# Strassen's seven products for two thirds of a transformer's down projection

## The chip, the core and the metric

The kernel runs on one core of a Trainium2 chip. The core has a matrix engine (TensorE, PE in the profile; its weight loads are shown as PEld), VectorE (DVE), ScalarE (ACT), GpSimd (POOL), a queue engine (SyncE, SP), and 16 DMA engines that move data between memory (HBM) and the core's own memories SBUF and PSUM. The metric is the device time of one execution in microseconds (us).

## The reference

An encoder of two layers over 512 tokens and 16 meta tokens, width 1024. Each layer is a feed-forward block, a mixer (gated linear attention beside grouped-query attention) and a second feed-forward block:

```python
def swiglu(x, w_gate, w_up, w_down):
    return (jax.nn.silu(x @ w_gate) * (x @ w_up)) @ w_down
...
    for l in range(DEPTH):
        h = h + 0.5 * swiglu(rmsnorm(h, norm_gains[l, 0]),
                             ffn_w_gate[l, 0], ffn_w_up[l, 0], ffn_w_down[l, 0])
        h = h + mixer(rmsnorm(h, norm_gains[l, 1]), w_in[l], ...)
        h = h + 0.5 * swiglu(rmsnorm(h, norm_gains[l, 2]),
                             ffn_w_gate[l, 1], ffn_w_up[l, 1], ffn_w_down[l, 1])
    return rmsnorm(h, final_norm)[:, N_META:]
```

The change is in the four feed-forward blocks. Their hidden width is 2816, so that `w_gate` and `w_up` are 1024 x 2816 and `w_down` is 2816 x 1024; all is float32.

## The kernel before

**Layout and precision.** Activations lie transposed: 128 features on the partitions, tokens along the row (528, and 512 in the last block, where the meta tokens are dropped). The residual `h` is eight such tiles. Each operand of a matmul is split into a part rounded to the matrix engine's float32r format (`hi`) and the remainder (`lo`); a product is three matmuls, hi x hi, hi x lo and lo x hi.

**Weights.** The class `Weights` holds one plan of all loads in the order of use. SP loads a slab of 128 x 1024 (512 KB) up to nine loads ahead; `make` casts it to `whi` on ScalarE (L238) and takes the remainder `wlo` on VectorE (L239), three or four slabs ahead of use, in four buffers each.

**A feed-forward block** (`ffn`, L507) goes through the hidden width in 11 pairs of 256 features, in groups of 4, 4 and 3 pairs (`GROUPS`). `ffn_steps` (L50) writes its order out by hand.

For a pair, gate and up are computed by Strassen's method in Winograd's form: the weights of the pair are cut into four blocks, the tokens into two halves, and seven block products ("P" steps, 1 to 7) take the place of eight. A product has 24 matmuls (L531). The products need sums of weight blocks. `Weights.sums` makes them with DMAs: ScalarE negates a block (L184), and GpSimd's queue issues transfers that add to a tile in SBUF (L189). s3 is block 21 less block 11, s2 is block 22 plus s3, s4 is s2 less block 12, s1 is block 21 plus block 22; they serve products 7, 6, 3 and 5. Their tiles lie in two pools, `wsa` (three buffers, for s3 and s4) and `wsb` (two, for s2 and s1). The products run one pair into the next: 1 and 2 of the next pair stand between 7 and 4 of this one.

ScalarE and VectorE put the products together in snapshots (L537) and sums (L545, L553, L560). `hidden` (L563) scales by the norm's factor (L571), takes the Silu, multiplies by up (L577) and splits the result into hi and lo (L392, L393).

**The down projection** ("D" steps, `down`, L580) follows each group: for each of eight output tiles the 2 x 4 (or 2 x 3) hidden tiles of the group are multiplied with tiles of `w_down`, three matmuls each, in two halves of 264 tokens (in the last block one of 512). With four pairs that is 8 x 8 x 3 x 2 = 384 matmuls. So that TensorE needn't wait for the last pair's hidden tiles, the first four output tiles leave these for later (`HELD`). The accumulated tile is scaled by the norm's factor (L494) and added to `h` (L503): 16 VectorE instructions a group.

**Around it.** `Norm` makes the operands of the next block as soon as a tile of `h` is done. In the first block of each layer the output tiles of the third group feed the mixer, in the others the next block or the ending (L1057), which works in halves of the tokens. The order on each engine comes from a scheduler that follows the order of the program, but may bring an instruction forward that has all it needs.

Of the kernel before, what the change touches and what calls it, by code (L numbers as in the profile page):

```python
# [41 lines left out]
GROUPS = (4, 4, 3)  # L42
LATE = 5
HELD = 4
OPENING = ((0, 0), 0), ((0, 0), 1)
PLACE = {p: i for i, p in enumerate("1256743")}
# [3 lines left out]
def ffn_steps(opening):  # L50
# [4 lines left out]
    for g, n in enumerate(GROUPS):  # L55
# [6 lines left out]
        for i in range(n):  # L62
# [8 lines left out]
        steps += [("D", g, m, 0, 2 * n - 2) for m in range(2, HELD)]  # L71
        steps += [("D", g, m, 2 * n - 2, 2 * n) for m in range(HELD)]
        steps += [("D", g, m, 0, 2 * n) for m in range(HELD, KC)]
# [4 lines left out]
def weight_plan():  # L78
# [8 lines left out]
    def ffn(l, f):  # L87
        for step in ffn_steps((l, f) == (0, 0)):
            if step[0] == "P":
                plan.append(("op", (l, f)) + step[1:])  # L90
            else:
# [38 lines left out]

PLAN = weight_plan()
COLUMN, NSLAB = slab_columns(PLAN)
NPAIR = FF // P // 2
# [18 lines left out]
class Weights:  # L152
# [18 lines left out]
    def dram(self, f, i, name):  # L171
        return self.win[((f[0] * 2 + f[1]) * NPAIR + i) * 4 + ("11", "12", "21", "22").index(name)]

# [102 lines left out]
def build(tc, ctx, xt, wts, win, par, w2, const, umask, out):  # L276
# [10 lines left out]
    slots = {n: pool("s_" + n, b) for n, b in dict(g=16, t=6, rs=2).items()}  # L287
# [27 lines left out]
    def slot(tag, dtype=F32, n=None):  # L315
        return slots[tag].tile([P, T], dtype, tag=tag, name=nm(tag))[:, : n or live[0]]

# [71 lines left out]
    def split(src, tag_hi, tag_lo):  # L389
        n = src.shape[-1]  # L390
        hi, lo = slot(tag_hi, F32R, n), slot(tag_lo, F32R, n)
# [32 lines left out]
    class Norm:  # L424
# [58 lines left out]
        def rs(self):  # L483
# [6 lines left out]
            return rs  # L490
# [5 lines left out]
    def add_to_h(m, acc, rs, f):  # L496
        if rs is None:
            for pv, cut in acc.parts:
                V.tensor_tensor(cut(h(m)), cut(h(m)), pv, ALU.add)
        else:  # L500
# [6 lines left out]
    def ffn(l, f, norm, done, following):  # L507

        x, rs, n = norm.x, None, live[0]
        w = n // 2  # L510
        pools = open_pools("left", psum=("s2",), c=2, snap=3, s2=2)
        made, hid, sums = {}, {}, {}

        def product_of_pair(p, product):
# [19 lines left out]
            def snapshot(name):  # L534
                t = slots["snap"].tile([P, T], F32, tag="snap", name=nm("snap"))[:, :n]
                st[name] = v2(t)
                copied = S.copy(st[name], acc).ins  # L537
                W.behind = copied

            if product == "1":  # L540
                snapshot("p1")
            elif product == "2":
                c = slots["c"].tile([P, 4 * T], F32, tag="c", name=nm("c"))[:, : 4 * n]
                st["c"] = c.rearrange("p (j q c) -> p j q c", j=2, q=4)
                V.tensor_tensor(st["c"][:, :, 0], st["p1"], acc, ALU.add)  # L545
            elif product == "6":
                snapshot("q")
            elif apart:
                S.copy(st["c"][:, :, 2], acc)
                st["apart"] = True  # L550
            elif product == "7":
                snapshot("r")
                V.tensor_tensor(st["c"][:, :, 3], st["r"], st["Z"][:, :, :w], ALU.add)  # L553
                if "apart" in st:
                    V.tensor_tensor(st["c"][:, :, 2], st["c"][:, :, 2], st["r"], ALU.add)
# [3 lines left out]
            elif product == "3":  # L559
                V.tensor_tensor(st["c"][:, :, 1], st["q"], acc, ALU.add)  # L560
                hidden(st, p, 0)

        def hidden(st, p, m):  # L563

            c = st["c"]
            t, u = [c[:, j, 2 * m : 2 * m + 2].rearrange("p q c -> p (q c)") for j in range(2)]
# [6 lines left out]
            if pending:  # L573
                with after(prev_act[0]):
                    pending.pop()()
            for _, ud, _, us, cs in cuts:
                V.tensor_tensor(ud, t[:, cs], us, ALU.mult)  # L577
            hid[2 * p + m] = split(u, "g", "g")
# [623 lines left out]
```

## Time and profile before

| What | Value |
|---|---|
| runs, median (3 runs) | 2235.04 us (2234.63 to 2238.08) |
| profiled execution, first to last instruction | 2233.2 us |
| mean granted TensorE clock | 0.998 |
| TensorE, VectorE, ScalarE busy | 2196.7, 1519.1, 1195.1 us |
| read from HBM | 264.77 MB |
| the two mixers, roughly | 390 to 770 us and 1500 to 1870 us |

The span is that of the one execution that was profiled; the profile gives no other time for it, and the runs above are separate executions. In the rows of the profile, "L404 PE MATMUL ss<-g,whi" means line 404, engine, operation, written tile, read tiles. A mean in ns is that of one instruction. Where "idle before" stands, it is the time that the engine did nothing ahead of these instructions, with what ended it.

### The profile page before, as it was taken

The page shows a single profiled execution, that of the slowest core. Times are in us where ns is not written, and L with a number is a line of the kernel's source. Part 1 is how long each engine was busy: PE and PEld are TensorE (multiplying, and loading weights), DVE is VectorE, ACT ScalarE, POOL GpSimd, SP SyncE. Part 2 cuts the span into 40 slices and gives each one's busy share as a digit, 9 for nine tenths or more (in the row PEclk, how much of TensorE's full clock was granted, in tenths as well). Part 3 has the DMA queues.
Part 4 walks back from the last instruction along what each step waited for, and adds up shares of the span by engine and source line. Part 5 has one row for each costly group of instructions (what it writes and reads, how often), then busy time and mean ns, then how long its engine had stood idle before and what let it go on. Part 6 is the DMA issues. An engine that isn't in the chain of part 4 may idle for free.

```text
span 2233.2 us, 39696 instructions
## 1 busy us (share of the span) xinstructions
PE 2196.7 (98%) x16506; PEld 2091.9 (94%) x16506; DVE 1519.1 (68%) x2413; ACT 1195.1 (54%) x1771; POOL 154.2 (7%) x180
## 2 busy tenths in 40 slices
PE   7999999999999999999999999999999999999998
PEld 7999999989999999999999999999788888989897
DVE  7657567586876666565686565675878767756667
ACT  8536355354784564453575353553557836636453
POOL 1111010000000010101011110100000001101010
PEclk9999999999999999999999999999999999999999
DMA  9768563212113486776768686632121146868672
GB/s 275 206 157 221 152 164 106 76 53 72 48 39 114 133 201 168 171 195 154 198 152 207 154 204 167 165 109 77 54 79 48 48 123 156 221 161 207 168 182 67
DMA packets 88612, 315.58 MB, mean 141 GB/s; under 512 B 9840, under 2 KB 12272, under 8 KB 88432
## 3 DMA queue, kind: packets, MB, share of 16 engines
q1 hardware_dynamic: 61136, 218.26, 29.2%
q0 software_dynamic: 25344, 92.29, 23.2%
q8 instruction: 130, 2.13, 0.4%
q10 hardware_dynamic: 1952, 2.50, 0.3%
q14 instruction: 50, 0.41, 0.1%
HBM read 264.77 MB, written 2.10 MB: 120 GB/s over the span
## 4 chain that ended last, share of the span: by engine, by line
PE 79%; DVE 8%; DMA 6%; ACT 5%; issue 2%; SPq 0%; POOL 0%; DVEq 0%; ACTq 0%; POOLq 0%
PE ss L531 30%; PE ss L404 26%; PE mm L404 13%; DMA w<-win 4%; PE sm L404 2%; DVE wlo L239 2%; DMA s<-w 2%; PE sm L916 1%; ACT whi L238 1%; PE ss L891 1%; PE ss L410 1%; ACT t L387 1%; PE sm L932 1%; PE ss L892 1%; PE sm L933 1%
## 5 line engine op out<-in xcount | busy, mean ns | idle before, releaser
L531 PE MATMUL ss<-xc,whi 128*128 128x264 f32 (+1 forms) x4928 | 902.8, 285 | 13.3 <-ACT whi L238 7.4
L531 PEld LDWEIGHTS ss<-xc,whi 128*128 128x128 f32 x4928 | 766.2, 189 | 17.2 <-ACT whi L238 7.6
L531 PE MATMUL ss<-xc,wlo 128*128 128x264 f32 (+1 forms) x2464 | 701.8, 285 | 3.4 <-DVE wlo L239 3.4
L404 PE MATMUL ss<-g,whi 128*128 128x264 f32 (+2 forms) x2692 | 496.8, 300 | 1.6 <-ACT g L392 0.9
L531 PEld LDWEIGHTS ss<-xc,wlo 128*128 128x128 f32 x2464 | 465.7, 189 | 5.2 <-DVE wlo L239 5.0
L404 PEld LDWEIGHTS ss<-g,whi 128*128 128x128 f32 x2692 | 391.6, 188 | 19.1 <-ACT g L392 1.6
L404 PE MATMUL mm<-x,whi 128*128 128x264 f32 (+1 forms) x1712 | 384.7, 315 | 0.0
L239 DVE TENSOR_TENSOR wlo<-w,whi 128x1024 fp32r<-128x1024 f32 (+1 forms) x221 | 268.0, 1217 | 157.2 <-ACT whi L238 157.1
L238 ACT CAST whi<-raw 128x1024 fp32r<-128x1024 f32 x190 | 199.3, 1049 | 246.6 <-PE mm L404 97.5
L238 ACT CAST whi<-w 128x1024 fp32r<-128x1024 f32 (+1 forms) x221 | 229.8, 1046 | 160.0 <-PE ss L404 88.0
L404 PE MATMUL ss<-g,wlo 128*128 128x264 f32 (+2 forms) x1346 | 312.5, 300 | 0.0
L404 PEld LDWEIGHTS mm<-x,whi 128*128 128x128 f32 x1712 | 278.5, 188 | 16.5 <-issue 1.0
L239 DVE TENSOR_TENSOR wlo<-raw,whi 128x1024 fp32r<-128x1024 f32 x190 | 232.0, 1221 | 74.3 <-ACT whi L238 73.9
L404 PE MATMUL mm<-x,wlo 128*128 128x264 f32 (+1 forms) x856 | 266.3, 316 | 0.0
L404 PEld LDWEIGHTS ss<-g,wlo 128*128 128x128 f32 x1346 | 215.8, 188 | 8.2
L537 ACT COPY snap<-ss 128x528 f32<-128x528 f32 (+1 forms) x132 | 78.4, 594 | 221.0 <-PE ss L531 221.0
L404 PEld LDWEIGHTS mm<-x,wlo 128*128 128x128 f32 x856 | 159.7, 188 | 8.4 <-issue 0.7
L494 DVE SCALAR_TENSOR_TENSOR t<-ss,rs 128x528 f32<-128x528 f32 (+1 forms) x93 | 64.5, 701 | 125.5 <-PE ss L404 125.4
L239 DVE TENSOR_TENSOR wlo<-s,whi 128x1024 fp32r<-128x1024 f32 x88 | 107.5, 1222 | 32.9 <-ACT whi L238 32.9
L184 ACT ACTIVATE s<-w 128x1024 f32<-128x1024 f32 x88 | 92.1, 1057 | 53.2 <-DMA w<-win 37.7
L189 POOL DMA_DIRECT2D w<-win x44 | 38.9, 884 | 984.1 <-DMA w<-win 539.9
L238 ACT CAST whi<-s 128x1024 fp32r<-128x1024 f32 x88 | 92.5, 1051 | 0.0
(246 smaller groups left out, 2570.8 us busy)
## 6 DMA issues: line engine op xcount, KB each, us to landing
w<-win SPq DMA_DIRECT2D x219, 512.0 KB, 4.5
raw<-wts SPq DMA_DIRECT2D x190, 512.0 KB, 3.4
s<-win POOLq DMA_DIRECT2D x44, 512.0 KB, 7.1
w<-s POOLq DMA_DIRECT2D x44, 512.0 KB, 5.5
w<-win POOLq DMA_DIRECT2D x44, 512.0 KB, 5.9
s<-w POOLq DMA_DIRECT2D x44, 512.0 KB, 8.0
h<-xt SPq DMA_DIRECT2D x3, 528.0 KB, 6.1
out<-h ACTq DMA_DIRECT2D x4, 256.0 KB, 2.4
```

What stands on the lines that cost most here:

```text
L184: self.nc.scalar.activation(t, w, AF.Copy, scale=-1.0)
L189: self.nc.gpsimd.dma_start(t, src, accum_op=ALU.add)
L238: nc.scalar.copy(hi[:, cs], w[:, cs])
L239: nc.vector.tensor_tensor(lo[:, cs], w[:, cs], hi[:, cs].bitcast(F32), ALU.subtract)
L387: prev_act[0] = S.activation(*args, **kw).ins
L404: TE.matmul(acc.half[i][:width], lhs, rhs[:, acc.spans[i]], start=first, stop=last)
L410: TE.matmul(a, weights, x[:, hs], start=True, stop=True)
L494: V.scalar_tensor_tensor(cut(dst[rows]), pv[rows], -0.5 * f, cut(rs[rows]), ALU.mult, ALU.mult)
L531: TE.matmul(acc[:, j], a[:, j, k], b[:, at], start=bool(begin and k == 0 and i == 0), stop=k == len(x) - 1 and i == 2, skip_group_check=no ...
L537: copied = S.copy(st[name], acc).ins
L891: TE.matmul(s[:n, i, :HF], lhs, kh[:, hs], start=True, stop=False)
L892: TE.matmul(s[:n, i, :HF], lhs, kl[:, hs], start=False, stop=True)
```

## The change

In groups 0 and 1 of each feed-forward block (`FAST = 2`) the down projection is computed with Strassen's seven products too; group 2 stays as it was. The eight hidden tiles of a group become four quarters (each of the two halves of a pair, for each half of the tokens), 128 x 4 x 264. Each half of the output's features (a "quad", `dq` 0 and 1, `QUADS = 2`) takes seven products of 24 matmuls ("S" steps).

```diff
+            if not more and g < FAST:
+                rest = [("S", g, 0, c, 2) for c in "125"]
+                steps += [("O", g, 0), ("P", p, "7"), ("P", p, "4"), ("S", g, 0, "1", 1), ("P", p, "3")]
+                steps += [("S", g, 0, c, 1) for c in "25"] + [("O", g, 1)] + rest
+                steps += [("S", g, *t, 3) for t in zip(AB, "16273465734")]
+                continue
```

Products 1, 2 and 5 of the first quad take the first three pairs first (part 1) and the last pair later (part 2); the other eleven products follow, of both quads in turn (`AB`). The blocks of `w_down` come through the same loads, sums and pools as those of gate and up (`NOP` blocks in place of `NPAIR`); six slabs that were plain loads remain for group 2.

`hidden` no longer splits the tiles of these groups, but multiplies into the four quarters `raw`. The operands of a product are made when it is near: differences of quarters on VectorE, a cast on ScalarE, a remainder on VectorE. "O" steps make those of 1, 2 and 5 (and 6), the others follow the products of the second quad:

```diff
+        def operand(g, c, ks=slice(0, 4)):
+            src = raw[g][{"1": 0, "2": 2, "5": 0, "6": 0, "7": 1, "3": 3, "4": 2}[c]]
...
+                S.copy(hi, src[:, ks])
+                V.tensor_tensor(lo, src[:, ks], hi.bitcast(F32), ALU.subtract)
...
+        def difference(g, into, a, b, ks=slice(0, 4)):
+            V.tensor_tensor(r[into][:, ks], r[a][:, ks], r[b][:, ks], ALU.subtract)
...
+        def operands_behind(g, dq, c):
+            if (dq, c) == (1, "1"):
+                difference(g, 1, 1, 3)
+                operand(g, "7")
+            elif (dq, c) == (1, "2"):
+                operand(g, "3")
+                difference(g, 2, 2, 0)
+                operand(g, "4")
```

Each product, as it stands in PSUM (6, 7 and 4 go on in the sum of 1, and 3 in that of 5), is added to the `h` tiles that it belongs to, without scaling:

```diff
+                to = hall[:, 4 * dq + m : 4 * dq + m + 3 : 2, q * w : (q + 1) * w]
+                V.tensor_tensor(to, to, acc, ALU.add)
```

For that `h` is brought to the scale of the unscaled products: early in the block each tile is multiplied by `up`, the inverse of the norm's factor, and behind the third group by the factor and one half.

```diff
+                up = slot("rs")
+                V.scalar_tensor_tensor(cut(up), mv, EPS, cut(rs), ALU.add, ALU.mult)
...
+                if step[1] in (2, 3) and step[2] in "6574":
+                    m = next(risen)
+                    V.scalar_tensor_tensor(h(m), h(m), -1.0, up, ALU.mult, ALU.mult)
...
-            t = slot("t")
-            scaled(t, acc, rs, f)
-            V.tensor_tensor(h(m), h(m), t, ALU.add)
+    def lower_h(m, rs, cs=None):
+        return V.scalar_tensor_tensor(h(m, cs), h(m, cs), -0.25, rs[:, cs], ALU.mult, ALU.mult)
```

The pools follow: `g` has 8 tiles of double width in place of 16 (the mixer's gates come in twos), `c` four of half the width in place of two, and the snapshots are written into the `c` tiles, so that their own pool goes.

```diff
-    slots = {n: pool("s_" + n, b) for n, b in dict(g=16, t=6, rs=2).items()}
+    slots = {n: pool("s_" + n, b) for n, b in dict(g=8, t=6, rs=2).items()}
...
-        pools = open_pools("left", psum=("s2",), c=2, snap=3, s2=2)
+        pools = open_pools("left", psum=("s2",), c=4, s2=2)
```

More of the change, by code (lines that the diff above doesn't have):

```diff
@@ L42 @@
 GROUPS = (4, 4, 3)
+FAST = 2
+QUADS = 2
 LATE = 5
@@ L171, in dram @@
     def dram(self, f, i, name):
[L172 removed]
+        return self.win[((f[0] * 2 + f[1]) * NOP + i) * 4 + ("11", "12", "21", "22").index(name)]
     def block(self, f, i, name, pool=None, tag="raw"):
@@ new lines, in fast_down @@
+        def fast_down(g, dq, c, part):
+            last = sum(GROUPS[: g + 1]) - 1
+            kinds = ("ss", "s2") if last % 2 == 0 else ("s2", "ss")
+            st = made.setdefault(("S", g, dq), {})
+            where = {"2": "Y", "5": "Z", "3": "Z"}.get(c, "X")
+            begin = c in "125"
+            if part != 2:
+                if begin:
+                    st[where] = pair(kinds[{"Y": 0, "Z": 1, "X": dq}[where]] == "s2")
+                st["w"] = st.get("w", {})
+                st["w"][c] = W.op((l, f), NPAIR + QUADS * g + dq, c, ahead=AHEAD_MADE - 1)
+            acc = st[where][:, :, :w]
+            hi, lo = st["w"][c]
+            xs = sets[g, c]
+            for k in {1: range(3), 2: range(3, 4), 3: range(4)}[part]:
+                for j in range(2):
+                    for i, (a, b) in enumerate(((hi, 0), (hi, 1), (lo, 0))):
+                        TE.matmul(acc[:, j], a[:, j, k], xs[b][:, k], start=bool(begin and k == 0 and i == 0),
+                                  stop=k == 3 and i == 2, skip_group_check=not begin)
+            if part == 1:
+                return
+            st["w"].pop(c)
+            for m, q in {"1": [(0, 0)], "2": [(0, 0)], "5": [(1, 1)], "6": [(0, 1)], "3": [(0, 1)], "7": [(1, 1)],
+                         "4": [(1, 0)]}[c]:
+                to = hall[:, 4 * dq + m : 4 * dq + m + 3 : 2, q * w : (q + 1) * w]
+                V.tensor_tensor(to, to, acc, ALU.add)
+            if dq == 1:
+                sets.pop((g, c))
+            operands_behind(g, dq, c)
```

154 lines of the change are left out of this document (107 added, 47 removed).

## The prediction

> **What bounds the kernel now.** I read the page's first part, then the waits of TensorE, then the chain of waits inside the feed-forward blocks, then the busy time of the two stages that the change touches.
>
> ```profile
> span 2233.2 us, 39696 instructions
> PE 2196.7 (98%) x16506; PEld 2091.9 (94%) x16506; DVE 1519.1 (68%) x2413; ACT 1195.1 (54%) x1771; POOL 154.2 (7%) x180
> ...
> PE ss L531 <- ACT whi L238: 7.4, 1, 7.4
> PE ss L531 <- DVE wlo L239: 3.4, 7, 0.7
> PE ss L531 <- ACT snap L537: 2.9, 3, 1.0
> ...
> 800.84 52.95 PE ss L531 x432
> 853.79 4.37 PE ss L404 x36
> ...
> 871.32 37.99 PE ss L404 x312
> 909.30 73.19 PE ss L531 x600
> ...
> 1965.25 36.22 PE ss L404 x156
> ...
> 2127.66 51.06 PE ss L531 x432
> ```
>
> The first two rows are the span and the busy time of each engine, the next three the longest waits of TensorE, the rest stretches of the chain (start, length, matmuls). L531 is the gate and up product, L404 in these places the down projection. TensorE waits some 7 us before its first matmul and then hardly at all: in a feed-forward block it runs from matmul to matmul. So a matmul taken away is worth its own pace, provided that what feeds the others keeps up. The paces: 37.99 / 312 = 121.8 ns in the down projection (264 columns), 73.19 / 600 = 122.0 ns in the products; in the last block 36.22 / 156 = 232.2 ns (512 columns) and 51.06 / 432 = 118.2 ns (256 columns).
>
> ```profile
> 871.32:909.30 37.98, 37.98 (x314) 37.98 (x314) 20.51 (x26) 12.07 (x13) 3.47 (x4) 1.00 0.64 167
> 909.30:982.49 73.19, 73.19 (x603) 73.19 (x602) 46.33 (x58) 40.16 (x50) 9.63 (x11) 1.00 0.79 197
> 778.00:853.00 75.00, 73.69 (x597) 73.25 (x598) 53.12 (x72) 48.93 (x65) 9.61 (x11) 1.00 0.80 203
> ```
>
> These are stretches by engine (PE, PEld, DVE, ACT, POOL busy, then clock, DMA share, GB/s): a down projection, the products behind it, an opening. In the down projection VectorE is busy 20.51 of 37.98 us and the DMA share falls to 0.64; in the products it is 0.79. The down projection is where VectorE and the DMA queues have air, and the change spends that air.
>
> **TensorE's gain.** A group of four pairs has 8 x 8 tiles of three matmuls in two halves, 384 matmuls; the seven products take 2 x 7 x 4 x 2 x 3 = 336. Three blocks: 384 x 0.1218 - 336 x 0.1220 = 46.77 - 40.99 = 5.8 us a group, 34.7 us for six groups. The last block has 192 matmuls of 512 columns now and 336 of 256 then: 44.58 - 39.72 = 4.9 us, 9.7 us for two. Sum **44.4 us**, if nothing waits.
>
> **VectorE in the new stage.**
>
> ```profile
> L239 DVE TENSOR_TENSOR wlo<-w,whi 128x1024 fp32r<-128x1024 f32 x219 | 266.7, 1221 | 157.2 <-ACT whi L238 157.1
> L553 DVE TENSOR_TENSOR c<-snap,ss 128x528 f32<-128x528 f32 x33 | 23.3, 705 | 47.2 <-ACT snap L537 47.2
> L393 DVE TENSOR_TENSOR g<-c,g 128x528 fp32r<-128x528 f32 x66 | 46.6, 707 | 19.6 <-ACT g L392 18.9
> ...
> 111.67 0.42 DVE L577 TENSOR_TENSOR c<-c,ss 128x264 f32<-128x264 f32 x1
> 112.01 0.43 DVE L577 TENSOR_TENSOR c<-c 128x264 f32<-128x264 f32 x1
> 112.49 0.70 DVE L560 TENSOR_TENSOR c<-snap,ss 128x528 f32<-128x528 f32 x1
> 113.23 0.71 DVE L571 SCALAR_TENSOR_TENSOR c<-c,rs 128x528 f32<-128x528 f32 x1
> 113.86 1.22 DVE L239 TENSOR_TENSOR wlo<-raw,whi 128x1024 fp32r<-128x1024 f32 x1
> 114.99 0.70 DVE L393 TENSOR_TENSOR g<-c,g 128x528 fp32r<-128x528 f32 x1
> 115.61 0.70 DVE L577 TENSOR_TENSOR c<-c 128x528 f32<-128x528 f32 x1
> ```
>
> Grouped durations (mean ns behind the bar), then single instructions in order. From start to start a weight remainder takes 1.13 us (113.86 to 114.99), a 528-wide operation 0.62, a 264-wide one 0.34, and 0.74 where the next needs its result (112.49 to 113.23). The 1056-wide operations are new: between one 1024-wide remainder (1.22) and two 528-wide ones (1.41); I take 1.25, 1.17 from start to start, since length and not the number of rows sets these durations. The add of a PSUM pair into two strided rows of h lies between L553's 0.70 and two 264-wide ones (0.85); I take 0.70, as the source is the same.
>
> A stage needs 14 remainders, 14 adds to h, three low halves and one difference made in two pieces (0.90 + 0.35) and seven 1056-wide operations: 15.8 + 8.7 + 5.0 + 8.2 = 37.7 us on VectorE, beside 41.0 us of matmuls. That fits, but not at each place. Behind the last gate product VectorE has, in its order, the PSUM sum 0.74, the scaling 0.63, a remainder 1.13, two products of 264, a low half and a difference of 264 (1.4), a 1056-wide difference 1.17, a low half 0.35, an add to h 0.62, a remainder 1.13, the difference for product 6 at 1.17, two adds 1.24 and the low half of product 6's operand 1.25: 10.8 us. TensorE has 80 matmuls ahead of product 6's first, 9.8 us. **It waits about 1.1 us there**, and by the same count 0.4 us in front of product 4 of the first quad: 1.5 us a stage. With the upper ends (1.41 and 0.85) it is 14 x 0.15 + 7 x 0.16, 3 us more.
>
> ```profile
> L238 ACT CAST whi<-w 128x1024 fp32r<-128x1024 f32 x219 | 228.7, 1050 | 160.0 <-PE ss L404 88.0 <-DMA w<-win 43.1 <-PE ss L531 18.2
> ```
>
> ScalarE needs 14 casts, four negations of the same length and operands of 7.4 casts' length, 25.4 x 1.05 = 27 us of 41, and is no bound by itself; but its casts stand in one queue with the Silu of the last pair, which leads to the next part.
>
> **The weight sums.** The down weights now come as blocks with sums, as the gate weights do: per quad four loads and four accumulating transfers.
>
> ```profile
> w<-win SPq DMA_DIRECT2D x219, 512.0 KB, 4.5
> s<-win POOLq DMA_DIRECT2D x44, 512.0 KB, 7.1
> w<-s POOLq DMA_DIRECT2D x44, 512.0 KB, 5.5
> w<-win POOLq DMA_DIRECT2D x44, 512.0 KB, 5.9
> s<-w POOLq DMA_DIRECT2D x44, 512.0 KB, 8.0
> ...
> 838.84 0.86 POOL L189 DMA_DIRECT2D s<-w  x1 [2.61 <-DMA w<-s]
> 843.17 1.05 ACT L238 CAST whi<-w 128x1024 fp32r<-128x1024 f32 x1 [1.48 <-DMA w<-win]
> ...
> 965.55 0.87 POOL L189 DMA_DIRECT2D w<-win  x1 [2.23 <-DMA w<-win]
> 969.95 0.88 POOL L189 DMA_DIRECT2D s<-w  x1 [3.54 <-ACT whi L238]
> 975.23 1.05 ACT L238 CAST whi<-w 128x1024 fp32r<-128x1024 f32 x1 [4.83 <-DMA w<-win]
> ```
>
> The issue table (last number: median us from issue to landing), then the end of the products of a first and a second group: ScalarE already waits 1.48 and 4.83 us there for a sum. TensorE does not feel it, because the products leave three weights in hand. In the new stage the sum for product 5 of the first quad may load only when the last pair's s4 has landed (the buffer pool wsb has two). In the first group: s4 issued 838.84, + 8.0, + load 4.5, + 0.9 behind the other sum on POOL, + 5.9 = 858.1. Product 5 of the last pair ends at 853.79; behind it come 90 matmuls (11.0 us) to the end of the last gate product and 18 more; ScalarE comes to this sum 2.9 us before that end (its cast's buffer comes free with product 4, 4.9 us before, and two operations of 1 us stand ahead of it), at 861.9. It is 4 us early. In the second group: 969.95 + 19.3 = 989.3 against 982.49 + 11.0 - 2.9 = 990.6, 1.3 us early; with a landing like 965.55 to 975.23 (9.7 us instead of 5.9) it is 2.5 us late. What it blocks: ScalarE's queue, in it the Silu of the last pair's gate, on it VectorE's whole row above, and so TensorE, one for one. I take 0.5 us a stage for the first groups, 1.5 for the second: 8 us in all.
>
> The Trainium skill, DMA: Bandwidth & Descriptors, section "Anatomy of one DMA — SWDGE (gpsimd) path", gives 2.0 us plus the bytes at 436 GB/s for a transfer issued on POOL; my estimate from it is 3.2 us for 512 KB. By that no sum could be late and the forecast would fall by these 8 us; the trace differs, 5.5 to 8.0 us, since these accumulate and share the 16 engines, and the trace decides.
>
> Till now a down projection (share 0.64) let the queues run ahead before the next group's products; the new stage asks for as much as the products do (0.79). The first sums of the second and third groups come with less lead: between 0 and the 2.9 us of one product, eight times. I take 0.75 us, nearer the lower end, because TensorE did not wait at 975.23 either; 6 us.
>
> **What else moves.** The residual is scaled up in the opening (eight operations of 0.62 us and one for the factor) and down at the end of the third group, where it replaces the scaling of the sum one for one, as it does in the ending. In the opening VectorE is busy 53.12 of 75.00 us and weights are made three products ahead, so most of it hides; bounds 0 and two operations ahead of a remainder, 1.2 us; I take 0.5, four times, 2 us. The low halves of the hidden tiles no longer made in the products (0.62 on VectorE, about as much on ScalarE, twice a pair) gain nothing, because TensorE is already unbroken there. Snapshots now go straight into the c tiles and the g tiles come in twos; in the mixer the order on VectorE and ScalarE stays as it was. I count these nothing; the 24 matmuls of the next product hide them, and without that cover each would cost its 0.6 us.
>
> **The sum.** 44.4 - 8 x 1.5 - 8 - 6 - 2 = 16.4 us saved: 2233.2 - 16.4 = 2216.8 us of span. The median of the runs shown, 2235.04, lies 1.84 us above the span; so **2219 us**.
>
> **Rivals.** *The sums set the pace (slower).* If the chain in front of product 5 takes the worst rows rather than the medians (9.7 instead of 8.0 and of 5.9, and both loads one behind the other at 9.0), it is 29.3 us instead of 19.3. Then the sum is 6.2 us late in the first group and 8.7 in the second, and TensorE waits 7.7 and 10.2 us for gains of 5.8 and 4.9: 2235 + 4 x 7.7 + 4 x 10.2 + 8 - 44.4 = 2270. Halfway there, 3 and 6 us late, it gives 4 x 4.5 + 4 x 7.5 + 14 + 2 = 64 us against 44.4: **2255**. It decides from some 4 us of lateness a stage. For it: the waits of 1.48 and 4.83 us, and that the relief of the down projection goes. Against it: the same chain is 1 to 4 us early by medians. *VectorE eats it (no change).* With two thirds of the upper ends a stage waits 1.5 + 2 us, and with the other 16 us the gain is 44.4 - 28 - 16: **2235**. Against it: a 1024-wide row costs far less than two of 528. *Only the arithmetic (faster).* No sum is late: 44.4 - 12 gives **2203**; with VectorE on time too, 2191. For it: three weights in hand, and products that ran unbroken at a share of 0.79. That the change leaves TensorE's work as it is can be excluded: the counts of matmuls follow from the instructions that it builds.
>
> **How the numbers follow.** Forecast 0.44, sums late 0.29, VectorE 0.12, arithmetic alone 0.15. A measurement of this kernel can tell 0.2%, 4.5 us, from no change. Faster: 0.43 + 0.15 = 0.58. Same: 0.01 + 0.08 = 0.09. Slower: 0.29 + 0.04 = 0.33. The forecast's own range is 2208 to 2230. The whole range goes from 2198, between the arithmetic alone and no wait at all, to 2258, just past the halfway case; beyond both I leave some 2 in 10.
>
> **What would show it.** In the chain of the changed kernel a stage should be 336 matmuls in 42 to 45 us (41.0 without a wait). TensorE's waits should name the low half of product 6's operand at about 1 us, once a stage, and the low half of product 4's. VectorE should be busy over 85% of the stage. ScalarE's wait for a sum at the stage's start should be under 1 us in the first group and about 2 in the second; if it is 4 or more, the slower rival is right. If the products behind a stage no longer run at 122 ns a matmul, the queues and not VectorE are the new bound. The prediction is wrong if TensorE waits more than 5 us a stage, or nowhere.

## The result, and the profile after

The changed kernel takes **2299.62 us** (median of four runs, 2298.66 to 2299.84), the kernel before 2234.84 on the same chip (2233.93 to 2238.08): a ratio of 1.0285, 95% interval 1.0273 to 1.0297. It is slower by 64.8 us, where 16 us less were forecast; the time lies above the predicted range. The profiled execution has a span of 2297.8 us.

From the first part of the changed kernel's page (span, busy time of the engines) and from its chain of waits by engine:

```profile
span 2297.8 us, 40260 instructions
PE 2196.7 (96%) x16506; PEld 2090.2 (91%) x16506; DVE 1648.7 (72%) x2571; ACT 1289.5 (56%) x1867; POOL 210.4 (9%) x244
...
PE 46%; DMA 26%; DVE 14%; ACT 8%; issue 4%; POOL 0%; SPq 0%; ACTq 0%; POOLq 0%; DVEq 0%
```

TensorE is busy as long as before, 2196.7 us, though it has fewer columns to do; what that hides comes below. A quarter of the chain is now transfers. The longest waits of TensorE (who waited for whom, us in total, times, longest):

```profile
PE ss L559 <- ACT c L563: 26.6, 18, 3.5
PE ss L559 <- DVE wlo L253: 12.4, 21, 0.8
PE ss L559 <- ACT whi L252: 10.8, 9, 7.4
PE ss L673 <- ACT g L634: 9.5, 7, 1.8
```

L559 is the product of a pair, L673 the new product of the down projection. The longest wait isn't in the new stage at all, but in the gate and up products, for ScalarE's snapshots (L563). The stretches by engine (PE, PEld, DVE, ACT, POOL busy with instructions in brackets, clock, DMA share, GB/s) show the same; first a stage, then the second group's products, then a stage:

```profile
104.90:147.20 42.30, 40.50 (x321) 39.26 (x320) 36.16 (x44) 23.32 (x26) 6.20 (x8) 1.00 0.88 218
147.10:231.40 84.30, 79.10 (x628) 78.05 (x626) 49.84 (x63) 42.64 (x52) 12.94 (x15) 0.98 0.85 204
240.00:284.30 44.30, 41.81 (x322) 40.78 (x321) 37.10 (x44) 25.30 (x28) 6.33 (x8) 0.96 0.86 212
```

The second group's products ran at 122 ns a matmul before; here 624 of them take 84.3 us, 135 ns. Why, is read from one place in them. First ScalarE in order of time (start, length, in brackets the idle time before and what ended it), then TensorE:

```profile
217.85 1.05 ACT L252 CAST whi<-w 128x1024 fp32r<-128x1024 f32 x1 [6.35 <-DMA w<-win]
...
226.03 0.59 ACT L563 COPY c<-ss 128x528 f32<-128x528 f32 x1
```

```profile
226.67 0.70 PE L559 MATMUL ss<-xc,whi 128*128 128x264 f32 x2 [3.52 <-ACT c L563]
```

ScalarE stands 6.35 us in front of a cast whose sum hasn't landed. Behind it in its queue are a negation, a cast, two Silu (the second also waits for VectorE, which stands behind the same cast), an operand and the snapshot that TensorE needs: TensorE stops for 3.52 us. And the chain of waits around it is a relay of adding transfers (start, length):

```profile
172.10 10.07 DMA s<-w
...
182.19 4.35 DMA w<-win
...
187.75 9.56 DMA s<-win
...
197.34 9.56 DMA s<-w
...
206.97 4.76 DMA w<-win
...
212.99 7.22 DMA s<-w
...
220.26 8.99 DMA s<-win
...
230.52 9.36 DMA w<-win
...
239.96 1.06 ACT whi L252
```

s4 takes in s2 (s<-w); when that has landed, s2's buffer is free and a load for s1 goes into it (w<-win at 182.19 and 206.97), and behind that load GpSimd issues s1's adding transfer. Two links of this chain are not as the view has them. In this stretch GpSimd issues a transfer 0.65 us or more behind a landing that it waited for, and 0.40 us behind a negation of ScalarE; the s<-w at 197.34 and the s<-win at 220.26 come 0.03 and 0.05 us behind the landing named, and 0.40 us behind the ends of two negations, at 196.94 and 219.86. The negations stand behind casts of s1 that waited for s1's adding transfer, 4.89 us and, as above, 6.35 us:

```profile
194.93 1.05 ACT L252 CAST whi<-w 128x1024 fp32r<-128x1024 f32 x1 [4.89 <-DMA w<-win]
195.89 1.05 ACT L198 ACTIVATE s<-w 128x1024 f32<-128x1024 f32 x1
```

So the relay runs through ScalarE. The transfers also take longer than the medians of before (last number, issue to landing):

```profile
w<-win SPq DMA_DIRECT2D x299, 512.0 KB, 5.5
s<-win POOLq DMA_DIRECT2D x60, 512.0 KB, 8.0
w<-s POOLq DMA_DIRECT2D x60, 512.0 KB, 5.6
w<-win POOLq DMA_DIRECT2D x60, 512.0 KB, 7.5
s<-w POOLq DMA_DIRECT2D x60, 512.0 KB, 8.7
```

**Half clock.** Three stretches around that stop, by engine as above:

```profile
223.42:226.80 3.38, 0.13 (x1) 0.13 (x2) 2.10 (x4) 2.17 (x4) 0.00 (x0) 1.00 1.04 291
226.80:230.25 3.45, 3.45 (x17) 3.45 (x17) 3.42 (x5) 3.22 (x4) 0.37 (x1) 0.51 0.30 82
235.00:240.00 5.00, 5.00 (x43) 5.00 (x42) 1.53 (x2) 0.92 (x2) 1.12 (x2) 1.00 1.02 220
```

TensorE does nearly nothing for 3.38 us; the next 3.45 us are granted at 0.51 of the clock, and 17 matmuls fill what would hold 28. They count as busy. A stop needn't be that long to be followed by half clock: the half-clock rows of this trace begin on a grid of 3.41 us, and of the pieces of that grid at full clock (from 20 us to the last matmuls) the twelve in which TensorE was busy 1.69 us or less were each followed by half clock, and none with 1.80 us or more was. The mean granted clock over the span is 0.989, before it was 0.998: 2297.8 x 0.011 = 25 us of the span withheld against 2233.2 x 0.002 = 4. By this estimate some 20 of the 65 us are this second price of the stops.

### The profile page after: what moved, and what is told of

It reads as the page before. It is cut to its first block, busy times and chain, and to the rows that moved or that the text cites. A ratio compares the mean times of both kernels' runs of the same rounds, so it can differ in the third digit from the quotient of the medians.

```text
span 2297.8 us, 40260 instructions
## 1 busy us (share of the span) xinstructions
PE 2196.7 (96%) x16506; PEld 2090.2 (91%) x16506; DVE 1648.7 (72%) x2571; ACT 1289.5 (56%) x1867; POOL 210.4 (9%) x244
## 4 chain that ended last, share of the span: by engine, by line
PE 46%; DMA 26%; DVE 14%; ACT 8%; issue 4%; POOL 0%; SPq 0%; ACTq 0%; POOLq 0%; DVEq 0%
DMA w<-win 14%; PE mm L426 12%; PE ss L426 9%; PE ss L559 9%; DMA s<-w 8%; PE ss L673 7%; DVE wlo L253 4%; DMA s<-win 3%; ACT whi L252 3%; PE sm L426 2%; ACT s L198 1%; PE sm L1034 1%; DVE g L639 1%; DVE h L681 1%; ACT t L405 1%
## 5 line engine op out<-in xcount | busy, mean ns | idle before, releaser
L559 PE MATMUL ss<-xc,whi 128*128 128x264 f32 (+1 forms) x4928 | 918.5, 288 | 40.6 <-ACT c L563 26.6
L559 PEld LDWEIGHTS ss<-xc,whi 128*128 128x128 f32 x4928 | 775.7, 191 | 48.7 <-ACT c L563 30.4
L559 PE MATMUL ss<-xc,wlo 128*128 128x264 f32 (+1 forms) x2464 | 708.4, 288 | 12.5 <-DVE wlo L253 12.4
L253 DVE TENSOR_TENSOR wlo<-w,whi 128x1024 fp32r<-128x1024 f32 (+1 forms) x301 | 365.8, 1218 | 290.6 <-ACT whi L252 289.9
L559 PEld LDWEIGHTS ss<-xc,wlo 128*128 128x128 f32 x2464 | 471.6, 191 | 17.3 <-DVE wlo L253 17.3
L252 ACT CAST whi<-w 128x1024 fp32r<-128x1024 f32 (+1 forms) x301 | 312.4, 1044 | 212.3 <-DMA w<-win 114.8
L673 PE MATMUL ss<-g,whi 128*128 128x264 f32 (+1 forms) x1280 | 242.3, 287 | 10.3 <-ACT g L634 9.5
L252 ACT CAST whi<-raw 128x1024 fp32r<-128x1024 f32 x126 | 132.1, 1048 | 156.5 <-PE mm L426 102.8
L673 PEld LDWEIGHTS ss<-g,whi 128*128 128x128 f32 x1280 | 200.6, 190 | 15.3 <-ACT g L634 11.1
L253 DVE TENSOR_TENSOR wlo<-raw,whi 128x1024 fp32r<-128x1024 f32 x126 | 153.9, 1221 | 57.6 <-ACT whi L252 56.8
L198 ACT ACTIVATE s<-w 128x1024 f32<-128x1024 f32 x120 | 126.6, 1057 | 109.4 <-DMA w<-win 96.9
L673 PE MATMUL ss<-g,wlo 128*128 128x264 f32 (+1 forms) x640 | 182.3, 285 | 0.0
L426 PE MATMUL ss<-g,whi 128*128 128x264 f32 (+2 forms) x900 | 168.4, 301 | 6.8 <-ACT g L414 5.9
L253 DVE TENSOR_TENSOR wlo<-s,whi 128x1024 fp32r<-128x1024 f32 x120 | 146.5, 1221 | 38.2 <-ACT whi L252 38.2
L426 PEld LDWEIGHTS ss<-g,whi 128*128 128x128 f32 x900 | 132.0, 188 | 14.0 <-ACT g L414 6.9
L563 ACT COPY c<-ss 128x528 f32<-128x528 f32 (+1 forms) x132 | 77.9, 590 | 113.3 <-PE ss L559 112.9
```

The source lines that it names most:

```text
L198: self.nc.scalar.activation(t, w, AF.Copy, scale=-1.0)
L252: nc.scalar.copy(hi[:, cs], w[:, cs])
L253: nc.vector.tensor_tensor(lo[:, cs], w[:, cs], hi[:, cs].bitcast(F32), ALU.subtract)
L426: TE.matmul(acc.half[i][:width], lhs, rhs[:, acc.spans[i]], start=first, stop=last)
L559: TE.matmul(acc[:, j], a[:, j, k], b[:, at], start=bool(begin and k == 0 and i == 0), stop=k == len(x) - 1 and i == 2, skip_group_check=no ...
L563: W.behind = S.copy(part(st, q), acc).ins
```

## The experiments

All ratios are to the kernel before, run beside them. "Stage" is the time from first to last of the 318 matmuls in a row that a stage has, mean of eight; "second group" that of its products, mean of four blocks. Both are added up from the start and end times of the traces.

| Run | us | ratio, 95% interval | stage | second group |
|---|---|---|---|---|
| kernel before | 2234.84 | 1 | none | 73.0 (600 matmuls) |
| changed kernel | 2299.62 | 1.0273 to 1.0297 | 44.0 | 85.3 (624) |
| e14, nothing added | 2208.92 | 0.9871 to 0.9904 | 40.8 | 75.7 |
| e1, stages' sums not added | 2267.21 | 1.0134 to 1.0165 | 40.8 | 84.4 |
| e2, third wsb buffer | 2249.3 | 1.0063 to 1.0096 | 43.1 | 77.9 |
| e5, fourth wsa buffer | 2323.31 | 1.0355 to 1.0412 | 44.6 | 84.9 |
| e6, s4 on GpSimd | 2284.68 | 1.0206 to 1.0248 | 46.7 | 75.7 |
| e9b, the same in the products alone | 2254.1 | 1.0075 to 1.0102 | 44.4 | 75.7 |
| e9, e9b and third wsb buffer | 2232.73 | 0.9984 to 1.0001 | 41.4 | 75.7 |
| e3, no group by block products | 2238.98 | 1.0015 to 1.0033 | none | 72.8 (600) |

**Where is it: in the stage, the buffers, the residual?** Four edits to the changed kernel:

```diff
     def sums(self, f, i, product, w):
+        add = self.add if i < NPAIR else lambda t, src: None
...
-            self.add(s3, self.dram(f, i, "21"))
+            add(s3, self.dram(f, i, "21"))
```

> The changed kernel with the four adding transfers of each of the 16 operand sets of the down projection left out (its sums stay the loaded or negated block, so the down projection of the first two groups is not the reference's; all loads, negations, casts and matmuls stay). Theory A (the chain of adding transfers through the few sum buffers is too slow when the stage needs sums as well): 2195 to 2225 us, the eight stages at 39 to 41 us instead of 41 to 45, the products behind them back near 122 ns a matmul, and no half-clock stretches. Theory B (VectorE's and ScalarE's operand work paces the stage): 2275 to 2300. Theory C (the loads' bytes alone are too many): 2240 to 2270.

```diff
-        pools = open_pools("left", wsa=3, wsb=2)
+        pools = open_pools("left", wsa=3, wsb=3)
```

> The changed kernel with three instead of two buffers for the sums that start as a load. Theory A: the loop through the two buffers is loosened, 2235 to 2280 us. Theory B and C: no change, 2294 to 2304.

```diff
-FAST = 2
+FAST = 0
```

> The changed kernel with no group's down projection by block products (FAST = 0): what stays of the change is the residual raised, added to out of PSUM and lowered again, and the paired hi and lo tiles. Theories A, B, C: the same as before within 8 us, 2228 to 2243. Rival D (the residual's arithmetic itself costs): over 2250.

The same line with 1:

> The changed kernel with the first group's down projection alone by block products (FAST = 1), so that a plain projection stands behind the second group's products. Theory A (a stage uses up the transfers' lead, a plain projection gives it back): 2222 to 2250 us, with the second group's products under 79 us. Rival (each stage costs by itself, whatever follows): half of the loss, 2260 to 2272.

e1: 2267.21 us, in the band of theory C. By engine, a stage and the products behind two stages:

```profile
108.10:149.20 41.10, 40.01 (x322) 39.20 (x321) 35.11 (x41) 23.12 (x26) 3.66 (x5) 1.00 0.58 157
...
914.30:999.90 85.60, 80.01 (x627) 78.95 (x626) 50.90 (x64) 42.48 (x52) 10.55 (x12) 0.96 0.80 199
```

The stages came back to 41 us with VectorE and ScalarE doing as much as ever, so theory B falls. But the products behind them stayed at 84.4 us: they don't inherit their lateness from the stage's own adding transfers.

e2: 2249.3 us. One buffer more brings back 50 of the 65 us: buffers matter, as theory A has it, though e1 doesn't bear out its picture of the stage as the culprit. The transfers are as many as in the changed kernel, so the second group's products of e2's third block answer a rival too, that the 16 DMA engines are simply too full:

```profile
1279.00:1355.00 76.00, 76.00 (x624) 75.88 (x623) 48.02 (x61) 42.50 (x52) 13.18 (x15) 1.00 0.93 229
```

They run at full pace, 122 ns a matmul, at a share of 0.93 and 229 GB/s; those of the changed kernel took 135 ns at 0.85 and 204.

e3: 2238.98 us, 5.9 above the kernel before beside it (2233.05). The raised residual, with the paired tiles, costs 3 to 7 us by the interval; rival D is out.

e4: 2263.53 us (1.0125 to 1.0159), in the rival's band and above theory A's: about half of the loss for half of the stages. The one sign of theory A that came is the second group's products under 79 us, at 77.7. Stretches of it: the second group's products behind a stage, and the third's behind a plain projection:

```profile
147.30:224.90 77.60, 75.32 (x604) 74.90 (x603) 47.01 (x58) 39.70 (x50) 10.49 (x12) 0.98 0.87 212
280.40:333.20 52.80, 52.80 (x435) 52.80 (x434) 32.48 (x40) 28.89 (x36) 6.09 (x7) 1.00 0.72 179
```

129 ns a matmul and 122.

**Which link of the relay?** The loop as I read it: s4's adding transfer, the wsb buffer that it frees, the load of s1 into it, s1's adding transfer, ScalarE's cast of s1, and behind that in ScalarE's queue the negation that begins the next s4. Edits: `wsa=4` instead of 3 (e5); s4 by one subtraction (e6):

```diff
-            s4 = self.negative(f, i, "s4", w)
-            self.add(s4, got[f, i, "6"])
+            s4 = self.long.tile([P, SLAB], F32, tag="wsa", name=f"s4_{f[0]}{f[1]}_{i}")
+            self.nc.gpsimd.tensor_tensor(s4, got[f, i, "6"], w, ALU.subtract)
```

with `wsb=3` beside it (e7); and with s2 added by `gpsimd.tensor_tensor` too (e8).

> The changed kernel with four instead of three buffers for the sums that start as a negated copy; the two for the sums that start as a load stay. Theory A2 (what turns slower than the matmuls of an operand set is the loop s4's adding transfer, the buffer that it frees, the load of s1 into it, s1's adding transfer, ScalarE's cast of s1 and behind it the next s4): a fourth buffer of the other kind isn't in that loop, 2288 to 2304 us. Rival (the number of buffers in all, or simply the memory between the transfers): like a third buffer of the loaded kind, 2240 to 2270.

> The changed kernel with one sum of four, s4, made by one subtraction on GpSimd instead of ScalarE's negated copy and an adding transfer; buffers as in the changed kernel. Theory A2: the loop loses its 9 to 10 us transfer against an operation of some 2.5 to 4 us, falls under the 20.5 us that a set's matmuls take, and the lead isn't used up any more: 2210 to 2240 us, the second group's products at 122 to 126 ns a matmul. Rival (each load waits for HBM and the 16 engines, whoever adds): over 2265. If GpSimd's operation slows VectorE or is itself slow (over 8 us): 2260 to 2300.

> s4 on GpSimd and a third buffer for the sums that start as a load. Theory A2: both ways to loosen the loop together bring what is left of it: 2208 to 2225 us, that is the time with no group by block products (2239) less the 44 us of matmuls, plus 2 us of operand waits a stage. Rival: not under the third buffer alone, 2249.

> As e7_s4_pool_wsb3, and s2 added on GpSimd too, so that only two adding transfers of four are left. Theory A2: no loop is left to loosen, so the same as e7_s4_pool_wsb3 within 6 us. If GpSimd contends with VectorE: slower than it by over 10 us. If the transfers' share was still in the way: faster by over 6 us.

e5: 2323.31 us, slower than either forecast. A buffer outside the loop gives nothing back; that it costs 24 us I can't explain fully. The largest pieces are 12 us in the first block's first products (67.6 us against 55.7) and 9 in the last block's third group of products (60.1 against 51.3). The edit also moved ScalarE's order: 11 negations stand directly in front of another one there, 2 in the changed kernel, and ScalarE's wait for blocks to negate grew. From the waits of the changed kernel, then of e5:

```profile
ACT s L198 <- DMA w<-win: 96.9, 30, 5.9
```

```profile
ACT s L198 <- DMA w<-win: 175.7, 51, 9.8
```

e6: 2284.68 us, above the theory's band and inside the one for a GpSimd operation that slows VectorE (the rival's, over 2265, takes it in too), and yet the second group's products are at 76.3 us in three blocks and 73.9 in the last, 122 and 118 ns: taking one transfer of four out of the loop freed them wholly. The loss moved into the stages, 46.7 us. VectorE's weight remainders in the stage from 244.6 to 292 us of e6, and GpSimd's new operation:

```profile
L253 DVE TENSOR_TENSOR wlo<-w,whi 128x1024 fp32r<-128x1024 f32 x11 | 18.1, 1644 | 7.6 <-ACT whi L252 7.6
```

```profile
L221 POOL TENSOR_TENSOR s<-w,w 128x1024 f32<-128x1024 f32 x60 | 163.9, 2732 | 206.1 <-DVE wlo L253 102.4 <-issue 51.8 <-ACT whi L252 22.1
```

The mean remainder takes 1644 ns there instead of 1221. Over the whole trace, by start and end times, the 62 remainders that lie for more than half of their time beside a GpSimd subtraction take 2470 ns on average, the 472 that touch none 1219. VectorE is slower while GpSimd subtracts, and the stage, unlike the products, has little VectorE time to spare (36.16 of 42.30 us busy in the changed kernel, 49.84 of 84.30 in the products). The Trainium skill, SBUF — State Buffer, section "Who interferes with whom", says that a VectorE instruction with two inputs in SBUF contends with a GpSimd instruction that reads SBUF; these rows agree.

e7: 2267.48 us (1.0131 to 1.0161), e8: 2310.53 us (1.0319 to 1.0363): both far above theory A2's bands, with stages at 45.1 and 46.3 us. e7 came out as its rival has it, not under the third buffer alone; e8 is 43 us slower than e7, as the condition on GpSimd and VectorE has it, though its stages hold only 9 of these 43 us. More sums on GpSimd is worse.

**So: GpSimd in the products alone.** The subtraction of e6 under `if i < NPAIR and (f, i) not in OPENING`, else the two lines of the changed kernel; e9 with `wsb=3`, e9b with 2. And a rival that blames ScalarE's queue, with only the negation moved:

```diff
-        self.nc.scalar.activation(t, w, AF.Copy, scale=-1.0)
+        self.nc.gpsimd.tensor_scalar(t, w, -1.0, None, ALU.mult)
```

> s4 on GpSimd for the operand sets of the products alone (not for the first two of the program, and not for the down projection's sets, which keep the adding transfer), and a third buffer for the sums that start as a load. Theory A2 with what e6_s4_pool showed (products at 122 ns, but VectorE's subtractions stretched by GpSimd's where the stage has no room): the second group's products at 76 to 77 us, the stages at 42 to 44 us, 2212 to 2232 us in all. Rival (the stages' own transfers are then late instead): over 2245.

> The same with two buffers for the sums that start as a load, as in the changed kernel. Theory A2: the products stay at 122 to 124 ns a matmul, the stages lose what the third buffer gave there: 2222 to 2250 us. Rival (the buffer is what counts): over 2260.

> The changed kernel with the two negated copies of a set made on GpSimd instead of ScalarE; all transfers and buffers as they are. Theory A3 (what hurts is ScalarE's queue: a negation that waits for its block holds the casts and snapshots behind it): 2225 to 2262 us, ScalarE's waits for loads at L198 gone and TensorE's waits for snapshots (26.6 us) under 10. Theory A2 (the loop of transfers is too long, whoever negates): 2280 to 2305, the waits move to the casts.

> The same with a third buffer for the sums that start as a load. Theory A3: 2205 to 2232 us. Theory A2: as with the third buffer alone, 2242 to 2256.

e9: 2232.73 us, just over its band and no different from the kernel before (0.9984 to 1.0001). A stage and the second group:

```profile
106.60:148.10 41.50, 40.22 (x322) 39.27 (x321) 33.90 (x40) 20.65 (x23) 7.83 (x7) 1.00 0.85 219
147.90:224.20 76.30, 76.30 (x628) 76.30 (x626) 54.85 (x64) 41.61 (x51) 18.98 (x15) 1.00 0.83 206
```

Compare the DMA shares with the changed kernel's: 0.85 and 0.83 against 0.88 and 0.85. The 16 engines carry nearly the same load in products that run at full pace, as e2 showed already; what held them up was who waits for whom.

e9b: 2254.1 us, over its band, with the products as free as in e9 and the stages at 44.4 us. The subtraction frees the products, and then the third buffer frees the stages.

e10: 2311.34 us (1.033 to 1.0363), e11: 2346.46 us (1.0484 to 1.053): both above all bands. In e10 the second group's products came down to 77.5 us, but the stages rose to 48.6; in e11 the products stood at 85.9 and the stages at 50.1, so that a third buffer on top gave nothing back. GpSimd's negation takes 3.1 us where ScalarE's takes 1.06 (L198, 1057 ns in the changed kernel):

```profile
L198 POOL TENSOR_SCALAR s<-w 128x1024 f32<-128x1024 f32 x120 | 368.1, 3086 | 280.3 <-DMA w<-win 175.9 <-DVE wlo L253 81.3 <-ACT whi L252 18.0
```

As a fix, theory A3 fails: with ScalarE's queue relieved, the time got worse. As an account of the products it isn't refuted, since the edit brings GpSimd's slower negations with it.

**What carries the loss, and does the lead matter?** e12 swaps two products in the order of the stage on top of e9 (`"16273465734"` becomes `"12673465734"`, with the quads to match), e13 sets `AHEAD_FETCHED = 7` in the kernel before, e14 makes `add` return at once in the changed kernel.

> The kernel of e9 (s4 on GpSimd in the products, three buffers) with the second quad's product 2 ahead of the first quad's product 6, so that product 6's operand, whose low half VectorE finishes late, is wanted 2.9 us later. If that operand is what keeps a stage at 41.0 to 42.5 us where 318 matmuls at 122 ns take 38.8: the stages at 39.2 to 40.5 us, TensorE's waits for L639 c (9.8 us in all) under 3, 2216 to 2226 us, under both kernels. If another operand is late next or the stage is bound elsewhere: 2228 to 2237, stages unchanged.

> The kernel before with the loads run 7 instead of 9 entries ahead of the matmuls. Theory (a plain projection, whose 8 loads last 38 us of matmuls, gives the transfers a lead of some 20 us, and the products of the next sets live on it): the same loop of transfers now starts with less, its products slow down although no stage is there, 2245 to 2290 us. Rival (the loop keeps up with the products by itself, and only a stage makes it late): 2232 to 2240.

> The changed kernel with every adding transfer left out, the products' too (both products and down projection of the first two groups are not the reference's; loads, negations, casts and matmuls stay). Theory: with no loop left, products at 122 ns a matmul, stages at the 41 us that the operands allow, 2205 to 2225 us. Rival (loads through few buffers suffice to make it late): over 2240, as in e1_sums_not_added (2267).

e14: **2208.92 us**, as expected of the theory. Same loads, casts, negations and matmuls; a stage and the second group:

```profile
103.50:144.50 41.00, 40.07 (x322) 39.24 (x321) 36.36 (x41) 23.52 (x25) 0.00 (x0) 1.00 0.38 126
144.30:220.60 76.30, 76.30 (x628) 76.30 (x626) 48.69 (x61) 42.80 (x51) 0.00 (x0) 1.00 0.37 122
```

The adding transfers cost the changed kernel 2299.6 - 2208.9 = 90.7 us. Loads through few buffers don't make it late, so theory C falls too.

e12: 2259.19 us (1.01 to 1.013), slower than e9 by 26. TensorE's wait for product 6's operand (line 639 there) fell from 9.8 us to 1.5. In its place came other waits; first e9's row, then e12's:

```profile
PE ss L677 <- DVE c L639: 9.8, 15, 0.9
```

```profile
PE ss L677 <- DVE wlo L257: 15.3, 8, 1.9
PE ss L677 <- ACT whi L256: 7.5, 8, 0.9
```

Now weights are late in the stage: another operand came next, as the second expectation has it, at a higher price than its 2228 to 2237 us: the stages rose from 41.4 to 45.0.

e13: 2233.23 us (0.9985 to 1.0005): no slower. My theory of the lead, counted in loads fetched ahead, is wrong. From the issue and landing times in the traces, the microseconds between the landing of s4 and its cast, for the four sets of the second group's products and the first of the third's, in the first block:

```
                          set 1   set 2   set 3   set 4   next group
kernel before, 9 ahead     20.5     8.4     7.7    13.7     21.3
kernel before, 7 ahead     26.8    19.4    13.9    17.5     26.1
changed kernel, 9 ahead    10.2     3.7     1.2    11.8     11.2
```

A plain projection does give the next group's first sums some 20 us, a stage gives 10, and over the first three sets of a group the margin shrinks; that part holds. But a shorter horizon gives more margin, not less. And s4's margin, never negative here, doesn't tell whether the products are late: in e2's third block, at full pace, it is 10.8, 4.4, 2.3 and 13.8 us. What tells the changed kernel from e2 and e9b is s1: in the second group's products of its first block ScalarE waits for s1's adding transfer 1.2, 4.9 and 6.4 us, more from set to set (3.1, 7.6 and 7.2 us in the third block), and in no second group of e2 or e9b over 1 us. In SP's queue a load that waits for a buffer holds back the ones behind it: from 173.98 to 182.19 no load is issued, until the s4 transfer above has landed (SP's waits at L193 for an s4 transfer to let go of a buffer add up to 334.3 us in the changed kernel, 43 times). To see whether that order alone is the cause, the horizon of 7 was put into the changed kernel (e15), into e2 (e16) and into e9 (e17).

> The changed kernel with the loads run 7 instead of 9 entries ahead, buffers as they are. In e13_before_fetch7 this changed no time but gave the fourth sum 14 to 19 us between its landing and its cast where the kernel before had 8. Theory (SP's queue is in order: blocks fetched 9 entries ahead wait there for a buffer in front of the loads that the sums start from, so the order of the issues, not the number of transfers, makes the sums late): most of the loss comes back, 2225 to 2260 us, the second group's products under 79 us. Rival (the loop through two buffers is too long in whatever order): 2280 to 2320.

> The third buffer for the sums that start as a load, and loads 7 entries ahead. Theory (queue order): 2212 to 2235 us, products at 122 ns, stages 41 to 42.5. Rival: as with the third buffer alone, 2242 to 2256, or slower.

> The kernel of e9 (2232.7) with loads 7 entries ahead. Its products are at 122 ns already, its stages at 41.0 to 42.5, so queue order can give back little there: 2220 to 2233. Rival (the stages' sums come later with a shorter horizon): over 2238.

e15: 2278.77 us (1.0172 to 1.0207), just under the rival's band; the second group at 78.6 us, the stages at 44.3. e16: 2262.05 us (1.0102 to 1.0151), slower than e2; e17: 2248.57 us (1.0048 to 1.0072), slower than e9. The order of the issues is worth 21 us in the changed kernel and 13 and 16 us the other way in the loosened ones. It is part of the price, not the whole cause.

## Why the prediction was wrong

**TensorE's gain, VectorE, the residual: right in size.** With nothing added the kernel takes 2208.9 us. The prediction's rival without late sums said 2203 (2205 with its own 2 us for the residual, which that sum leaves out). The stage is 41.0 us for 318 matmuls at 122 ns (38.8): 2.2 us of waits where 1.5 was worked out. What TensorE waits for longest in a stage of e14 is the low half of product 6's operand, as named, 0.91 us where 1.1 was worked out (TensorE in order of time):

```profile
115.09 0.39 PE L673 MATMUL ss<-c,whi 128*128 128x264 f32 x1 [0.91 <-DVE c L635]
```

VectorE is busy 36.36 of 41.00 us there, 89%, as forecast over 85%. The 2 us of "What else moves" were too few: the residual's part is 5.9 us by e3.

**The weight sums: the step that failed.** "I take 0.5 us a stage for the first groups, 1.5 for the second: 8 us in all" and "The first sums of the second and third groups come with less lead ... 6 us". Together 14 us; the runs show 90.7 (e14), less whatever the kernel before loses to its own sums. The forecast is 81 us off, and 77 of them are this step. Where it lies, as the difference of the changed kernel to e14 in stretches: stages 351.7 - 326.1 = 26 us, the second group's products 341.0 - 302.8 = 38, the other products 12, the rest in between. The largest part is where the prediction put 0.75 us a stage.

Two errors made that number. I followed one sum, s1 of the first quad, through its transfers, and found it in time by medians. But s1 waits for the last set's buffer, and the next negation for s1's cast, so the sets form a loop, and lateness adds up from set to set: ScalarE's waits for s1 grow from 1.2 to 6.4 us within one group. I read "ScalarE already waits 1.48 and 4.83 us" as a curiosity that TensorE didn't feel; it was a margin already spent. And the price of an empty margin isn't the lateness alone: ScalarE's queue holds a snapshot behind the late cast, and the stop takes half of the clock behind it.

**The slower rival had the mechanism, not the place or the price.** It said 2255, at worst 2270, with waits of 4.5 to 10 us in a stage. (The halfway sum is off: it adds 14 + 2 where the worst case adds 8, and by the worst case's terms it gives 56 us and 2247.) Its sign, ScalarE's wait of 4 us or more for a sum at a stage's start, came at the second groups' stages, 4.1 to 4.9 us, and not at the first groups', at most 2.1. But the stages themselves lost 3.5 to 6.5 us against 122 ns a matmul in three blocks, and the second group's products behind them 8 to 11 against e14.

**The signs.** "The products behind a stage no longer run at 122 ns" came true, and with it "the queues and not VectorE are the new bound". The band of 42 to 45 us is for 336 matmuls; the table's 44.0 us are 318 of them, and with the 18 ahead (2.2 us) a stage takes 46.2 us, over the band, where e14's takes 43.0. At 5.5 us above full pace a stage on average, the condition "more than 5 us a stage" for being wrong is met. Of the 5.5, by e14, 3.2 us come from the adding transfers and 2.3 from operands (44.0, 40.8 and 318 matmuls at 122 or 118 ns, 38.5).

**What stays open.** That the adding transfers carry the loss is shown (e14), and so is that it isn't the load of the DMA engines (e2). Three edits that loosen the loop (a third wsb buffer, s4 off the transfers, the negation off ScalarE) each bring the second group's products down, to 77.9, 75.7 and 77.5 us; a buffer outside it doesn't (84.9). That is why I take the loop for the cause in the products. Two runs don't fit it as it stands: with the first and the third edit together the products are at 85.9 (e11), and in e5 they are late though ScalarE waits for s1 over 1 us only twice in the four groups; there it waits for blocks to negate instead. So a late transfer at another place of ScalarE's queue seems to do the same, which no run separates. How the loop's length divides between the transfers, the buffers and SP's order is not settled (e13, e15 to e17), nor why e5 costs 24 us, nor what makes the stages late in e9b. e9 still spends 22 us of span more than e14, 5 of them in the stages and most of the others where the blocks open. No version that makes all the sums came under 2232.7; 2209 is what the rest of the change would allow.

## What to carry to other kernels

Before a stage is replaced by one that asks for more transfers, follow every sum over several rounds, not one sum through one: if the wait for any of them grows from round to round, the old stage was paying it back, and a new stage that doesn't will stop the matmuls in a place that the change doesn't touch. One sum's margin can shrink harmlessly, as s4's does in e2, while another's is the one that is late. Follow buffers round the loop (who frees the buffer that the first transfer waits for), and try one buffer more before moving work. A wait for data on ScalarE, which takes its queue in order here, is priced by what stands behind it in that queue.

## What the runs showed of the hardware

A stop costs TensorE again afterwards: the 3.45 us behind a stretch with 0.13 us of work were granted 0.51 of the clock. In the trace of the changed kernel such stretches add up to some 44 us of the span; e14, whose longest stop in the blocks and mixers is 1.6 us, has none from 20 us to its last 8 us. The Trainium skill, TensorE: Matmul & The Clock Gate, section "What's actually happening", gives half the clock after one idle window of about 3.4 us. The length agrees with the grid of 3.41 us; the window needn't be idle, though, since up to 1.69 us of work in it did not keep the clock.

Adding transfers of 512 KB took 5.6 to 8.7 us by medians, and the share of the DMA engines says little on whether they are in time: the products ran at full pace at 0.83 (e9) and 0.93 (e2), and at 135 ns a matmul at 0.85.

GpSimd's arithmetic has two prices: its own (2.7 us for a subtraction of 128 x 1024, 3.1 for a negation), and VectorE's subtractions beside it, 2470 ns instead of 1219 where they lie mostly under one of GpSimd's (e6).
